# Loading the first tile by rows and four later tiles by one DMA, in a contrast kernel

## The chip, the cores and the metric

One core of a Trainium2 chip. The metric is the device time of one execution in microseconds, as the median of several runs. One run of each kernel also left a profile. The experiments ran on two chips; a cost is always taken against the kernel before, run in the same rounds on the same chip (239.18 to 239.35 us).

## The reference

```python
# x: 16 x 3 x 512 x 512 float32, factor = 1.5
mean = np.mean(x, axis=(2, 3), keepdims=True)
return np.clip(mean + factor * (x - mean), 0, 1).astype(np.float32)
```

There are 48 images of 1 MB. 50.33 MB are read and 50.33 MB written, and the output of an image cannot begin before all of it has been summed.

## The kernel before

A tile is 128 rows of 8192 floats (32 KB), 4 MB, and holds four images on 32 partitions each. Twelve tiles pass through a ring of six buffers. VectorE sums one part of a row and ScalarE the rest; a small matmul adds up the rows of an image; VectorE scales and clips in place. Loads are issued from the SP queue (SyncE's), stores from the ACT queue (ScalarE's).

```python
P = 128; ROW = 8192; BUFS = 6; SHORT = 2048
FIRST = (SHORT, ROW - SHORT); SUM = 4352
# ... (pools, constants)
def load(t, c0=0, c1=ROW, n=1):
    b = t % BUFS
    src = bass.AP(tensor=x_f.tensor, offset=t * P * ROW + c0,
                  ap=[[ROW, P], [P * ROW, n], [1, c1 - c0]])
    nc.sync.dma_start(out=ring[:, b : b + n, c0:c1], in_=src)

def compute(t):
    # ... tensor_reduce, activation with accum_out, two matmuls into `shift`
    for n in FIRST if t == 0 else [ROW]:
        # ... tensor_scalar (scale, shift), tensor_scalar (clip)
        store(t, c, c + n)
        c += n

with tc.manual_schedule():
    load(0, c1=SHORT)
    load(0, c0=SHORT)
    load(1)
    load(2, n=2)
    load(4, n=2)
    for t in range(n_tiles):
        compute(t)
        if t + BUFS < n_tiles:
            load(t + BUFS)       # waits until the store of tile t has landed
```

## Time and profile before

| | before |
|---|---|
| time | 239.19 us (239.09 to 239.53, 3 runs) |
| span of the profiled run | 237.3 us |
| VectorE busy | 163.1 us (69%) |
| DMA engines | 9 tenths or more in 38 of 40 slices, 424 GB/s over the span |

The DMA row of the page tells how much of each fortieth of the span the sixteen DMA engines had a packet under way. The GB/s row below it tells what they moved. The lines stand in the prediction below.

### The profile page before, as it was taken

The page shows a single profiled execution, that of the slowest core. Times are in us where ns is not written, and L with a number is a line of the kernel's source. Part 1 is how long each engine was busy: PE and PEld are TensorE (multiplying, and loading weights), DVE is VectorE, ACT ScalarE, POOL GpSimd, SP SyncE. Part 2 cuts the span into 40 slices and gives each one's busy share as a digit, 9 for nine tenths or more (in the row PEclk, how much of TensorE's full clock was granted, in tenths as well). Part 3 has the DMA queues.
Part 4 walks back from the last instruction along what each step waited for, and adds up shares of the span by engine and source line. Part 5 has one row for each costly group of instructions (what it writes and reads, how often), then busy time and mean ns, then how long its engine had stood idle before and what let it go on. Part 6 is the DMA issues. An engine that isn't in the chain of part 4 may idle for free.

```text
span 237.3 us, 285 instructions
## 1 busy us (share of the span) xinstructions
PE 14.1 (6%) x48; PEld 12.0 (5%) x48; DVE 163.1 (69%) x38; ACT 43.2 (18%) x25; POOL 0.9 (0%) x9
## 2 busy tenths in 40 slices
PE   0010010001010001010010100100100100010000
PEld 0010010001010001010010100100100100010000
DVE  0079989048989328999989898891892795687000
ACT  2050230041050023050320504101400500500000
POOL 1000000000000000000000000000000000000000
DMA  7999999999999999999999999999999999999996
GB/s 297 410 442 442 421 442 359 456 439 441 442 436 414 403 431 442 442 442 442 436 442 436 414 409 425 442 442 442 442 436 442 436 420 403 425 442 442 442 442 265
DMA packets 3712, 100.66 MB, mean 424 GB/s; under 512 B 384, under 2 KB 384, under 8 KB 384
## 3 DMA queue, kind: packets, MB, share of 16 engines
q1 hardware_dynamic: 1840, 50.33, 49.7%
q10 hardware_dynamic: 1872, 50.33, 49.2%
HBM read 50.33 MB, written 50.33 MB: 424 GB/s over the span
## 4 chain that ended last, share of the span: by engine, by line
DMA 57%; DVE 29%; another core or an unknown queue 3%; PE 1%; SPq 1%; issue 0%; DVEq 0%
DMA ring<-in_x_dram 41%; DMA out_dram<-ring 16%; DVE sums L81 10%; DVE ring L91 9%; DVE ring L94 9%; PE bias L87 1%; SPq L76 1%; DVEq L91 0%
## 5 line engine op out<-in xcount | busy, mean ns | idle before, releaser
L81 DVE TENSOR_REDUCE sums<-ring 128x1 f32<-128x4352 f32 x12 | 56.2, 4683 | 45.7 <-DMA ring<-in_x_dram 45.7
L84 ACT ACTIVATE junk<-ring 128x3840 f32<-128x3840 f32 x12 | 40.8, 3403 | 163.3 <-DMA ring<-in_x_dram 107.5
L91 DVE TENSOR_SCALAR ring<-ring,bias 128x8192 f32<-128x8192 f32 (+2 forms) x13 | 54.1, 4163 | 8.9 <-PE bias L87 7.4
L94 DVE TENSOR_SCALAR ring<-ring 128x8192 f32<-128x8192 f32 (+2 forms) x13 | 53.3, 4099 | 0.4
L86 PE MATMUL bias<-sums,blockw 128*128 128x1 f32 x24 | 7.0, 361 | 190.8 <-ACT junk L84 190.8
L86 PEld LDWEIGHTS bias<-sums,blockw 128*128 128x128 f32 x24 | 6.0, 312 | 191.7 <-ACT junk L84 175.2
L87 PE MATMUL bias<-sums,blockw 128*128 128x1 f32 x24 | 7.0, 363 | 4.3 <-DVE sums L81 3.9
L87 PEld LDWEIGHTS bias<-sums,blockw 128*128 128x128 f32 x24 | 6.0, 311 | 5.3 <-DVE sums L81 5.0
L84 ACT ACTIVATION_READ_ACCUMULATOR junk<-ring 128x1 f32 x12 | 2.2, 186 | 0.0
L84 ACT ACT_TABLE_LOAD x1 | 1.3, 1283 | 0.7 <-PEq L129 0.7
L63 POOL MEMSET blockw<- 32x32 f32 x4 | 0.5, 117 | 0.2
L61 POOL MEMSET blockw<- 128x128 f32 x1 | 0.2, 204 | 0.3 <-POOLq L129 0.3
L129 POOL MEMSET const-bfloat16-1.0<- 128x1 bf16 x1 | 0.1, 111 | 0.0
L129 POOL MEMSET const-uint8-127<- 128x1 uint8 x1 | 0.1, 111 | 0.0
L129 POOL MEMSET const-float32-1.0<- 128x1 f32 x1 | 0.1, 108 | 0.0
L129 POOL MEMSET const-float32-0.0<- 128x1 f32 x1 | 0.1, 103 | 0.2 <-issue 0.2
## 6 DMA issues: line engine op xcount, KB each, us to landing
out_dram<-ring ACTq DMA_DIRECT2D x11, 4096.0 KB, 35.8
ring<-in_x_dram SPq DMA_DIRECT2D x7, 4096.0 KB, 49.7
ring<-in_x_dram SPq DMA_DIRECT2D x2, 8192.0 KB, 66.7
ring<-in_x_dram SPq DMA_DIRECT2D x1, 3072.0 KB, 11.7
out_dram<-ring ACTq DMA_DIRECT2D x1, 3072.0 KB, 28.2
ring<-in_x_dram SPq DMA_DIRECT2D x1, 1024.0 KB, 4.8
out_dram<-ring ACTq DMA_DIRECT2D x1, 1024.0 KB, 17.5
```

Of the source, the lines that this page charges most:

```text
L61: nc.gpsimd.memset(blockw, 0.0)
L63: nc.gpsimd.memset(blockw[a : a + ppi, a : a + ppi], wconst)
L76: nc.sync.dma_start(out=ring[:, b : b + n, c0:c1], in_=src)
L81: nc.vector.tensor_reduce(out=own[:, 0:1], in_=xt[:, 0:SUM], axis=mybir.AxisListType.X, op=Alu.add)
L84: nc.scalar.activation(out=junk, in_=xt[:, SUM:ROW], func=Act.Copy, accum_out=own[:, 1:2])
L86: nc.tensor.matmul(shift, blockw, own[:, 1:2], start=True, stop=False)
L87: nc.tensor.matmul(shift, blockw, own[:, 0:1], start=False, stop=True)
L91: nc.vector.tensor_scalar(out=part, in0=part, scalar1=factor, scalar2=shift, op0=Alu.mult, op1=Alu.add)
L94: nc.vector.tensor_scalar(out=part, in0=part, scalar1=0.0, scalar2=1.0, op0=Alu.max, op1=Alu.min)
L129: nc = _bacc.Bacc("TRN2", target_bir_lowering=False, num_devices=1)
```

## The change

The diff suggests a smaller first DMA, so that data may begin to flow earlier and in longer packets, and one issue for four tiles in place of two. The number of load issues before the loop stays five.

```diff
-    def load(t, c0=0, c1=ROW, n=1):
+    def load(t, p0=0, p1=P, c0=0, c1=ROW, n=1):
 ...
-            offset=t * P * ROW + c0,
-            ap=[[ROW, P], [P * ROW, n], [1, c1 - c0]],
+            offset=(t * P + p0) * ROW + c0,
+            ap=[[ROW, p1 - p0], [P * ROW, n], [1, c1 - c0]],
 ...
-        nc.sync.dma_start(out=ring[:, b : b + n, c0:c1], in_=src)
+        nc.sync.dma_start(out=ring[p0:p1, b : b + n, c0:c1], in_=src)
 ...
-        load(0, c1=SHORT)
-        load(0, c0=SHORT)
+        load(0, p1=HEAD, c1=SHORT)          # HEAD = 32
+        load(0, p1=HEAD, c0=SHORT)
+        load(0, p0=HEAD)
         load(1)
-        load(2, n=2)
-        load(4, n=2)
+        load(2, n=BUFS - 2)
```

The stores of tile 0 keep their two column parts.

More of the change, by code (lines that the diff above doesn't have):

```diff
@@ L13 @@
 SHORT = 2048
+HEAD = 32
 FIRST = (SHORT, ROW - SHORT)
```

## The prediction

Its sum came to 245.5 us: 239.19 - 0.1 + 1.6 = 240.7 us from numbers of the trace, and the rest (4.8 us) for a slower load of tile 0 by rows. The forecast of 244.6 us and its range contain it.

> **What bounds the kernel now.** I read the page from the top: engine shares, then the DMA rows of the forty slices, then the queues.
>
> ```profile
> span 237.3 us, 285 instructions
> PE 14.1 (6%) x48; PEld 12.0 (5%) x48; DVE 163.1 (69%) x38; ACT 43.2 (18%) x25; POOL 0.9 (0%) x9
> ...
> DMA  7999999999999999999999999999999999999996
> GB/s 297 410 442 442 421 442 359 456 439 441 442 436 414 403 431 442 442 442 442 436 442 436 414 409 425 442 442 442 442 436 442 436 420 403 425 442 442 442 442 265
> ...
> HBM read 50.33 MB, written 50.33 MB: 424 GB/s over the span
> ```
>
> VectorE is the busiest compute engine and works 69% of the time, while the DMA row shows 9 in every slice but the first and the last. So the sixteen DMA engines are the bound: 100.66 MB have to pass, and almost nothing else shows in the span. The records of single packets in the trace close the sum. A row of 32 KB takes 1.213 us on one DMA engine, one of 24 KB 0.912 us, one of 8 KB 0.309 us, at all times, with loads and stores mixed or not. A tile has 128 rows, 8 per engine, so a tile costs 8 x 1.213 = 9.7 us of every engine, and 12 loads and 12 stores cost 24 x 9.7 = 232.9 us. The first packet begins at 2.2 us and the first packets are slow (0.5 to 1 us lost); 2.2 + 0.7 + 232.9 = 235.8, and the last packet does end just above 236. The stream has no holes. The issues say when things arrive:
>
> ```profile
> out_dram<-ring ACTq DMA_DIRECT2D x11, 4096.0 KB, 35.8
> ring<-in_x_dram SPq DMA_DIRECT2D x7, 4096.0 KB, 49.7
> ring<-in_x_dram SPq DMA_DIRECT2D x2, 8192.0 KB, 66.7
> ring<-in_x_dram SPq DMA_DIRECT2D x1, 3072.0 KB, 11.7
> out_dram<-ring ACTq DMA_DIRECT2D x1, 3072.0 KB, 28.2
> ring<-in_x_dram SPq DMA_DIRECT2D x1, 1024.0 KB, 4.8
> ```
>
> A load of 4 MB needs 9.7 us alone but lands 49.7 us after its issue: transfers queue up, two or more deep. Last I read the timeline of VectorE, to see what it waits for:
>
> ```profile
> 12.96 4.69 DVE L81 TENSOR_REDUCE sums<-ring 128x1 f32<-128x4352 f32 x1 [12.96 <-DMA ring<-in_x_dram]
> ...
> 50.67 4.69 DVE L81 TENSOR_REDUCE sums<-ring 128x1 f32<-128x4352 f32 x1 [8.77 <-DMA ring<-in_x_dram]
> ...
> 218.17 0.34 ACTq L101 DMA_DIRECT2D out_dram<-ring  x1
> ```
>
> The first column is the start, the bracket the idle time before it. Tile 0 is there at 13.0, tiles 2 and 3 together at 50.7, tiles 4 and 5 together at 87.6 (the same row at that time, idle 8.2). Each tile then takes VectorE 4.69 + 0.65 (matmul) + 4.50 + 4.43 = 14.3 us. The last store is issued at 218.2, yet the span ends 19 us later, though one store alone needs 9.7: the store before it is still being written. So there is slack in compute even at the end. (Stores of tile 0 are issued at 20.9 and 27.6, of tile 1 at 41.9.)
>
> [...]
>
> **The change, part by part.** It removes nothing of the 100.66 MB and adds no instruction; five load issues stay five (3 + 1 + 1 in place of 2 + 1 + 2).
>
> First, packets of tile 0. Before, each engine had 8 x 0.309 + 8 x 0.912 = 9.77 us; now 2 x 0.309 + 2 x 0.912 + 6 x 1.213 = 9.72. That gains 0.05 us. A shorter first issue (32 rows instead of 128; the 128-row issues take 0.34 to 0.42 us) could bring the first packet forward by about 0.1 us. Compute of tile 0 waits for all three parts, so nothing starts early.
>
> [...]
>
> Third, the large load. Tiles 2 to 5 now share one semaphore. All engine time before their landing: first packet and slow start 2.7, six loads 6 x 9.7 = 58.2, and the stores of tiles 0 and 1, which are done before that (they landed at 56 and 76.5), 19.4: sum 80.3; with the spread of engines VectorE starts tile 2 at **81** instead of 50.7. That looks like 30 us lost, but the DMA engines have other work: loads 6 and 7 (buffers freed by the two stores) and then store 2, which is issued at 81 + 14.4 = 95.4. That is 3 x 9.7 = 29.1 us, up to 109.5. The next store is issued at 95.4 + 14.3 = 109.7, and the way from an issue to its first packet is 1.4 us (0.74 to 2.16 at the start): 111.1. Load 8, which waits until store 2 landed, comes at about 111.5. So the DMA engines stand still once, for **1.6 us**. After that a store comes every 14.3 us and releases a load; the two need 19.4 us of DMA time, so the DMA engines fall behind again and no further hole opens. VectorE runs through: 81 + 10 x 14.3 = 224 for the issue of the last store, some 2 us before the store ahead of it is finished. It is nearly the bound, but not quite.
>
> [...]
>
> **Rivals.** (a) *All hidden, or a gain at the start*: [...] 239 to 240. For it speaks that the total bytes are equal and that the page of the kernel before shows nothing but bytes; against it, that the stream has at most about 1 us of loss at its start to give back, so a gain of 2% (4.8 us) is out of reach. (b) *VectorE becomes the bound*: it starts tile 2 30 us later and has 143 us of work left; 224 + 1.4 + 9.7 + about 1.5 gives a span of 236.7, below the DMA's end. A delay of a few microseconds in the landing at 81 moves both alike; a stall of VectorE of over 2 us in the second half would show. This makes 241 to 243. [...]
>
> **Range and chances.** [...] I predict 244.6, with 240.0 to 248.6 for 8 in 10. The border of 2% is 243.97: slower 0.55, same 0.43, faster 0.02.
>
> **What would show it.** [...] Middle: VectorE idle from about 42 to 81 (plus the loss at the start) and hardly any idle after it. One dip in the DMA row some 28 us after that landing. End: the last store issued about 14 us before the span's end, not 19. The prediction is wrong if one DMA of 16 MB is cut up and releases tiles early, if engines drift apart so that holes add up, or if VectorE waits at the end.

## The result

| | before | after |
|---|---|---|
| time, median of 6 runs each | 239.10 us | 251.27 us (250.42 to 251.78) |
| span of the profiled run | 237.3 us | 249.5 us |

The ratio is 1.0503, with a 95% interval of 1.0483 to 1.0523: slower by 5%. (Ratios here are the mean time of one kernel's fast runs over that of the other's fast runs of the same rounds, so they differ a little from the ratio of the medians.) The direction was forecast, but the time lies above the stated range, which ended at 248.6.

The page of the changed kernel, its first line and its DMA rows:

```profile
span 249.5 us, 286 instructions
...
DMA  7997999999999999999989999999999999999996
GB/s 173 247 231 278 431 447 420 441 441 441 405 457 457 426 420 420 420 426 415 336 389 436 405 420 436 426 426 468 431 420 426 431 431 457 441 420 420 436 426 263
```

A reader of the DMA row alone sees no change: 9 nearly everywhere. The GB/s row shows two places. The first four slices (0 to 25 us) move about six tenths of what they moved before, and slices 20 and 21 (some 119 to 131 us) are low. The first place, in stretches of time that I chose, the kernel before and then the kernel after (the columns are stretch, length, busy time of PE, PEld, DVE, ACT and POOL, granted clock, share of time in which the DMA engines were busy, GB/s; a packet, which is one row's piece of a load or store, is counted whole in the stretch in which it starts, so a share can pass 1):

```profile
3.00:13.00 10.00, 0.00 (x0) 0.00 (x0) 0.04 (x1) 0.12 (x1) 0.00 (x0) 1.00 1.03 440
```

```profile
3.00:13.00 10.00, 0.00 (x0) 0.00 (x0) 0.00 (x0) 0.00 (x0) 0.00 (x0) 1.00 0.99 216
13.00:21.00 8.00, 0.00 (x0) 0.00 (x0) 0.00 (x0) 0.00 (x0) 0.00 (x0) 1.00 1.00 217
```

The DMA engines are equally busy (1.03 and 0.99), but they move 216 GB/s in place of 440. In the records of single packets, each of the 96 rows of 32 KB in tile 0 takes 2.2 to 2.6 us (1.21 nearly everywhere else). These packets begin in six bunches of sixteen, each bunch within 1.2 us: the sixteen engines go through the load in step. The issues of the changed kernel and its timeline, with the time to landing last in the first fence:

```profile
ring<-in_x_dram SPq DMA_DIRECT2D x1, 16384.0 KB, 87.5
ring<-in_x_dram SPq DMA_DIRECT2D x1, 3072.0 KB, 20.8
...
ring<-in_x_dram SPq DMA_DIRECT2D x1, 768.0 KB, 6.9
ring<-in_x_dram SPq DMA_DIRECT2D x1, 256.0 KB, 3.4
```

```profile
22.54 4.69 DVE L82 TENSOR_REDUCE sums<-ring 128x1 f32<-128x4352 f32 x1 [22.54 <-DMA ring<-in_x_dram]
...
90.10 4.69 DVE L82 TENSOR_REDUCE sums<-ring 128x1 f32<-128x4352 f32 x1 [38.08 <-DMA ring<-in_x_dram]
...
104.52 0.34 ACTq L102 DMA_DIRECT2D out_dram<-ring  x1
...
118.82 0.34 ACTq L102 DMA_DIRECT2D out_dram<-ring  x1
```

Tile 0 is complete at 22.5 us, 9.6 us later than before. The head (256 and 768 KB) lands at 8.0, and the other 96 rows land 14.4 us later (22.41 - 8.03). Tile 2 starts at 90.1 after VectorE idled for 38 us. Its store is issued at 104.5 and that of tile 3 at 118.8; around that time lies the second dip.

### The profile page after: what moved, and what is told of

Same layout as the page of the kernel before. It is cut to its first block, busy times and chain, and to the rows that moved or that the text cites. A ratio compares the mean times of both kernels' runs of the same rounds, so it can differ in the third digit from the quotient of the medians.

```text
span 249.5 us, 286 instructions
## 1 busy us (share of the span) xinstructions
PE 13.9 (6%) x48; PEld 12.0 (5%) x48; DVE 162.6 (65%) x38; ACT 43.2 (17%) x25; POOL 0.9 (0%) x9
## 5 line engine op out<-in xcount | busy, mean ns | idle before, releaser
L85 ACT ACT_TABLE_LOAD x1 | 1.3, 1283 | 22.5 <-DMA ring<-in_x_dram 22.5
```

What stands on the lines that cost most here:

```text
L85: nc.scalar.activation(out=junk, in_=xt[:, SUM:ROW], func=Act.Copy, accum_out=own[:, 1:2])
```

## The experiments

**1 and 2: each part alone.** The first kernel has the three-part load of tile 0 only, the second the one load of four tiles only.

```diff
 # e1_head_only, against the changed kernel
-        load(2, n=BUFS - 2)
+        load(2, n=2)
+        load(4, n=2)
 # e2_large_only, against the kernel before
-        load(2, n=2)
-        load(4, n=2)
+        load(2, n=BUFS - 2)
```

> Only the three-part load of tile 0, tiles 2 to 5 in two loads as before. [...] tile 0 lands at about 22.5 us as in the changed kernel, 9.6 us later than before, and the time is 239.1 + 9.7 = 248.8 us. Rival (most of the 12 us comes from the late landing of the large load): 241 to 243 us.

> Only the one load of tiles 2 to 5, tile 0 in two column parts as before. Theory of the single hole: tile 2 starts at about 80 us, the DMA engines run dry once near 108 us, and the time is 239.1 + 1.6 to 2.5 = 240.7 to 241.6 us. Rival (the late start is what costs): 248 us or more. Rival (all hidden): 239.1 us.

Measured: 247.94 us for the head alone (ratio 1.0363) and 242.76 us for the large load alone (ratio 1.0149), against 239.35 for the kernel before on that chip. The costs are 8.6 and 3.4 us; their sum, 12.0, is nearly all of the 12.2 us of the whole change. Nothing shows that the parts depend on each other. In the first kernel tile 0 was complete at 22.5 us, as in the changed kernel. Its loss is 8.6 and not the 9.5 us by which tile 0 is late, and the packet records show why. Take what every packet needs above the usual time of its size, add it up and divide by sixteen engines. Up to 24 us this is 9.9 us in this kernel and 0.5 in the kernel before. From 24 to 104 us the kernel before loses 0.8 us to slow packets of its own and this kernel 0.05, which leaves a net loss of 8.7. The second cost more than I expected of the hole.

**3 and 4: is it which rows go together, or the row count?** Two loads of 64 whole rows each, once as lower and upper half, once as even and odd rows.

```diff
 # e3_halves, against e1_head_only
-        load(0, p1=HEAD, c1=SHORT)
-        load(0, p1=HEAD, c0=SHORT)
-        load(0, p0=HEAD)
+        load(0, p1=64)
+        load(0, p0=64)
 # e4_even_odd: the same two counts, with a step of 2 in the rows of both sides
+        load(0, p0=0, ps=2)      # out=ring[p0:p1:ps, ...], source step ps * ROW
+        load(0, p0=1, ps=2)
```

> Tile 0 as rows 0 to 63 and rows 64 to 127, whole rows of 32 KB, two loads; the rest as before. [...] tile 0 still takes twice 9.7 us, lands at about 22 us, time about 248.8 us, packets of about 2.4 us. Rival (few rows per load, 8 KB packets, a row count of 96, or a third issue are what is slow): packets of 1.2 us and 239 to 241 us.

> Tile 0 as the even rows and the odd rows, 64 rows each, both spread over partitions 0 to 127 [...]. [...] packets of 1.2 us, tile 0 at about 13 us, 239.1 us. [...] If the number of rows per load counts: as the halves.

Measured: 249.16 us for the halves (ratio 1.0416), 239.31 us for even and odd (ratio 1.0001, interval 0.9984 to 1.0017). The loads of 2 MB in each, halves first, then even and odd:

```profile
ring<-in_x_dram SPq DMA_DIRECT2D x2, 2048.0 KB, 18.1
```

```profile
ring<-in_x_dram SPq DMA_DIRECT2D x2, 2048.0 KB, 9.8
```

The number of loads, rows, bytes and packets is the same in both. Only which rows go together differs, and it makes all of the 9.8 us by which the halves are slower. A small row count or a third issue is not the cause.

**5 and 6: SBUF side or HBM side?** Both sides changed together so far: neighbouring partitions were filled from neighbouring rows of HBM. These two kernels separate them, at the price of a wrong result.

```diff
 # e13_rows_apart, against e4_even_odd: r0, rs are first row and step in HBM
+        load(0, p1=64, r0=0, rs=2)        # partitions 0..63   <- even rows
+        load(0, p0=64, r0=1, rs=2)        # partitions 64..127 <- odd rows
 # e14_parts_apart
+        load(0, p0=0, ps=2, r0=0)         # even partitions <- rows 0..63
+        load(0, p0=1, ps=2, r0=64)        # odd partitions  <- rows 64..127
```

> Wrong result on purpose (the images of tile 0 are mixed up). Tile 0 in two loads of 64 rows: partitions 0 to 63 from the even rows of HBM, 64 to 127 from the odd rows. If the SBUF side makes the half rate: tile 0 at about 23 us and 249 us, as the halves. If the addresses in HBM make it (a block of neighbouring rows): 239.3 us, as even and odd.

> Wrong result on purpose. The other way round: even partitions from rows 0 to 63 of HBM, odd partitions from rows 64 to 127. SBUF side: 239.3 us, tile 0 at about 13 us. HBM side: 249 us.

Measured: 249.04 us (ratio 1.041) and 239.52 us (ratio 1.0011), both with a wrong result (relative error 0.24). The stretch from 3 to 13 us, neighbouring partitions first, then partitions apart:

```profile
3.00:13.00 10.00, 0.00 (x0) 0.00 (x0) 0.00 (x0) 0.00 (x0) 0.00 (x0) 1.00 1.00 210
```

```profile
3.00:13.00 10.00, 0.00 (x0) 0.00 (x0) 0.00 (x0) 0.00 (x0) 0.00 (x0) 1.00 0.94 403
```

The half rate goes with the partitions that are written (210 GB/s for neighbours, 403 for partitions apart), not with the rows that are read. What in the hardware makes it is not shown.

**7 and 8: five loads, blocks against every fourth row.** The head of the changed kernel and three more loads of 32 rows, once as blocks of neighbours, once as every fourth row.

```diff
 # e12_quarters, against e1_head_only
-        load(0, p0=HEAD)
+        for r in range(HEAD, P, HEAD):
+            load(0, p0=r, p1=r + HEAD)
 # e10_step4: head from rows 0, 4, 8 ...
+        load(0, p0=0, c1=SHORT, ps=4)
+        load(0, p0=0, c0=SHORT, ps=4)
+        for r in range(1, 4):
+            load(0, p0=r, ps=4)
```

> Tile 0 in five loads: the head as in the changed kernel (8 and 24 KB of rows 0 to 31), then rows 32 to 63, 64 to 95, 96 to 127; tiles 2 to 5 as before. [...] half rate throughout, tile 0 at about 22.5 us, 248 to 249 us. If the 96 rows in one load were slow for their odd row count [...], the three 32-row loads are faster: 243 to 245 us.

> The same five loads, same counts and sizes, but every fourth row in each (rows 0, 4, 8 ... for the head, then those from 1, 2 and 3)[...]. [...] full rate, tile 0 at about 13 us, 239.1 to 239.6 us. If 32 rows per load, 8 KB packets or five issues are what is slow: 248 us as the quarters.

Measured: 248.79 us for the blocks and 240.94 us for every fourth row (ratio 1.0059). The blocks (212 GB/s from 3 to 23 us) behave like the 96 rows in one load (216 from 3 to 13), so it is not the count of 96. Every fourth row (410 GB/s from 3 to 13 us) gives back 7.9 us but not all: it missed its expectation by over 1 us. Tile 0 was complete at 14.9 us there, not at 13. By the packet records the first 8 us lose some 0.9 us more than in the kernel before (engines idle 0.4, slow packets 0.5), and the engines finish further apart at the end; why is open.

**9: both halves at once, on two queues.**

```diff
 # e6_two_queues, against e3_halves (load() has a new argument eng, nc.sync by default)
-        load(0, p0=64)
+        load(0, p0=64, eng=nc.scalar)
```

> Tile 0 as rows 0 to 63 on the load queue and rows 64 to 127 at the same time on the other queue; the rest as before. If the engines go through the two halves in step[...]: tile 0 at about 22 us, 248.8 us as the halves on one queue. If they fall out of step[...]: packets between 1.2 and 2.4 us, 240 to 245 us.

Measured: 248.23 us (ratio 1.0373), and tile 0 complete at 23.7 us. With both halves on offer at the same time, the packets still took over 2.3 us (228 GB/s from 3 to 23 us). The records show the engines in step: from 4 us on sixteen packets of the load queue begin within 1.3 us (at 3.9 to 5.0), then sixteen of the other queue (6.2 to 7.5), then again sixteen of the first (8.6 to 9.8), and so on. So at one moment all sixteen engines wrote into one half of the partitions.

**10: the same split in the middle of the stream.**

```diff
 # e7_mid_split, against the kernel before
+                if t == 2:
+                    load(t + BUFS, p1=HEAD)
+                    load(t + BUFS, p0=HEAD)
```

> Tile 0 as before; tile 8, in the middle of the stream, is loaded as rows 0 to 31 and rows 32 to 127, with stores in turn beside it. [...] all of its extra 9.7 us stays, because the stream has no holes: 248.8 us. If the stores in between take the engines out of step [...]: less, 240 to 245 us.

Measured: 244.53 us (ratio 1.0236, interval 1.0198 to 1.0274): 5.3 us, six tenths of the cost at the start. The load's packets took 1.6 us in the mean, less than the 2.4 at the start; those of the stores beside them took up to 1.48 us. Together that is 4.1 us of each engine, and the rest is engines that finished apart. That the stores took the engines out of step fits this but is not shown.

**11 and 12: the large load.** One kernel fills the moment in which the DMA engines ran dry with an earlier part of tile 3's store; the other takes only three tiles in one load.

```diff
 # e5_large_fill, against e2_large_only
-        for n in FIRST if t == 0 else [ROW]:
+        for n in FIRST if t in (0, 3) else [ROW]:
 # e9_three_one, against e2_large_only
-        load(2, n=BUFS - 2)
+        load(2, n=3)
+        load(5)
```

> The large load alone (tile 0 as before), and the store of tile 3 in the two column parts that tile 0 has, so that its first 8 KB per row are ready some 6 us earlier and fill the moment in which the DMA engines ran dry. Theory of the hole: the 1 us of idle at 110 us goes, what the queues lose when each starts again stays, 241.5 us against 242.8. Rival (VectorE's late start is the bound): no change, 242.8 us.

> Tile 0 as before; tiles 2 to 4 in one load of 12 MB and tile 5 alone. Theory of the hole: tile 2 starts near 70 us, its store follows before the DMA engines run dry, no hole, 239.1 to 239.5 us. Rival (every large load costs in proportion to the delay of VectorE): about half of the 3.4 us, 240.8 us.

Measured: 240.50 us with the hole filled (ratio 1.0055), and 238.99 us with three tiles and one (ratio 0.9987, interval 0.9972 to 1.0002; no difference). In both, VectorE starts tile 2 far later than before (81.4 and 68.2 us against 50.7), so its late start is not the cost. The stretch of the dip, the large load alone and then with the hole filled:

```profile
104.00:108.00 4.00, 0.00 (x0) 0.00 (x0) 3.97 (x2) 0.00 (x0) 0.00 (x0) 1.00 0.95 410
108.00:112.00 4.00, 0.00 (x0) 0.00 (x0) 4.00 (x2) 1.49 (x1) 0.00 (x0) 1.00 0.61 262
112.00:116.00 4.00, 1.17 (x4) 1.00 (x4) 3.25 (x2) 2.00 (x2) 0.00 (x0) 1.00 1.24 393
116.00:120.00 4.00, 0.00 (x0) 0.00 (x0) 3.97 (x2) 0.00 (x0) 0.00 (x0) 1.00 0.82 352
```

```profile
108.00:112.00 4.00, 0.00 (x0) 0.00 (x0) 4.00 (x2) 1.21 (x1) 0.00 (x0) 1.00 0.86 365
112.00:116.00 4.00, 1.18 (x4) 1.00 (x4) 3.25 (x2) 2.29 (x2) 0.00 (x0) 1.00 1.17 455
116.00:120.00 4.00, 0.00 (x0) 0.00 (x0) 4.00 (x1) 0.00 (x0) 0.00 (x0) 1.00 0.94 367
```

In the first, a share of 0.61 at 108 to 112 us is the hole. By the packet records the engines were idle for 1.1 us on average. The store that then began was not slow at first (1.25 us a packet), but when the next load joined it, at 113 to 116 us, packets of both took up to 2.5 us. From 104 to 140 us slow packets cost each engine 2.0 us. With the hole filled the idle time is gone, and slow packets cost 0.8 us there. So filling took away 2.2 of the 3.4 us, the idle time and about half of the slow packets, more than the 241.5 us that I expected. What makes packets slow when a load joins was not tried.

**13 and 14: smaller loads, and both parts mended.**

```diff
 # e8_singles, against the kernel before
-        load(2, n=2)
-        load(4, n=2)
+        for t in range(2, BUFS):
+            load(t)
 # e11_step4_three_one: e10_step4 with load(2, n=3); load(5)
```

> Tile 0 as before, tiles 2 to 5 in four loads of their own instead of two of 8 MB. The stream has no hole in either, so 239.1 us, within 0.3%. If grouping matters in itself (fewer semaphore writes or issues), it is slower by some tenths.

> Both parts of the change mended: the head and the rest of tile 0 by every fourth row, tiles 2 to 4 in one load and tile 5 alone. Both costs should be gone: 239.0 to 239.4 us, the same as before. Nothing in the stream is left to gain but about 1 us of slow start.

Measured: 241.23 us for single loads (ratio 1.009, interval 1.0038 to 1.0142), a miss: 0.9% slower, where I expected nothing. The packet records show the sixteen engines drifting apart in it: the last load lands on the first and the last engine 3.4 us apart, against 1.8 us in the kernel before. The packets are no slower (0.1 us per engine in all); some 1.5 us are idle engines at the very end, which had finished before the last one. That the smaller loads make them drift is argued from this one profile. The mended kernel took 240.45 us (ratio 1.0052), a miss of 1 us: the large load costs nothing more there, but every fourth row still costs about what it costs alone (1.6 us). No version beat the kernel before clearly.

## Why the prediction was wrong

**The bound: right.** What the DMA engines lost came out at the end: in experiment 1 a net 8.7 us of slow packets per engine, and 8.6 us of time. The 8.6 and 3.4 us of experiments 1 and 2 add up to nearly the whole, 12.0 of 12.2. One reading was too smooth: rows of 32 KB do not take 1.213 us "at all times". In the kernel before, such packets of loads took up to 1.79 us while tile 0 was stored.

**The packets of tile 0: nothing gained.** The first packet began at 1.77 us, not earlier than the 1.74 of before. (The prediction had read 2.16 for this.)

**Tile 0 by rows: slower, as forecast, and its size was the step that failed.** The prediction made tile 0 4.8 us late (245.5 - 240.7); it was 9.6. In experiments 3 to 6 loads into neighbouring partitions were slow: 193 GB/s (3 to 23 us) and 210 (3 to 13 us) for neighbouring partitions, 403 and 419 (both 3 to 13 us) for partitions apart, with the same rows, bytes and packets. The head landed at 8.0 us. The 96 rows failed the estimate, which had let a part of them pass beside the others: their packets, divided by sixteen engines, took 14.5 us, twice the 7.3 us of six packets at 1.213, so 7.2 us more for them alone. All packets of the 96 rows were slow (2.2 to 2.6 us), so no part passed beside the others at the usual rate. Engines in step that write into one half at a time, as in experiment 9, would give this. For the 96 rows that is argued and not shown: the records do not say which row a packet carries, and one load across the middle alone (rows 32 to 95) was not tried. A rival that is cut had named a time of some 249, but the range stopped at 248.6.

**The large load: right in its course, too small in its size.** Alone, VectorE started tile 2 at 81.4 us (predicted 81), the stores of tiles 2 and 3 were issued at 95.8 and 110.1 (predicted 95.4 and 109.7), and there was one hole, near 110 us. But 1.6 us were predicted and 3.4 measured. The idle time was 1.1 us, less than predicted: the store's first packet came 0.8 us after its issue, not 1.4. The term that was left out is the slow packets after the hole, 2.0 us.

**VectorE as the bound: rightly rejected.** In the changed kernel VectorE runs without a wait for loads from 90 us on, and its last store is issued 16 us before the end of the span (predicted about 14).

With the two terms as measured, 8.6 and 3.4, the sum is 239.1 + 12.0 = 251.1, against 251.27. The prediction's own sum was 245.5; the 244.6 that it gave was lowered for the chance that the term for tile 0 does not apply.

## What to carry to other kernels

When DMA is the bound, look at GB/s and not at busy DMA engines alone: here, from 3 to 13 us, they were 99% busy at 216 GB/s, where the kernel before moved 440. Splitting the first load by every second row moved 419 GB/s in that stretch here, splitting it by columns 440, blocks of neighbouring partitions 216 or less: try the first two before blocks. A load of three tiles came later here than its user wanted it (VectorE started tile 2 at 68.2 us in place of 50.7) at no cost (238.99 us against 239.27); with four tiles it started at 81.4 us, the DMA engines ran dry for 1.1 us, and the kernel lost 3.4 us. So before merging loads, count how long other transfers fill the DMA engines until the user's first results arrive.
